# A two-layer attention and retention encoder: the first group's side work in half-round places, the prologue's list in another order, the first rotation read from PSUM

## The chip, the core and the metric

The kernel runs on one core of one Trainium2 chip. Its engines work side by side, each through its own instructions in order: TensorE (PE) multiplies matrices into PSUM, ScalarE (ACT) applies functions, VectorE (DVE) and GpSimd (POOL) do elementwise work, and SyncE (SP) issues the transfers. The metric is the device time of one execution in microseconds (us), lower is better. The kernel is built with its order of instructions written out by the program for PE, ACT, DVE and POOL; the order of SP is written out in the prologue and the first group's first part, and planned by the compiler behind it.

## What is computed

```python
def hybrid_layer(x, norm_gain, w_in, w_out, rel_bias, cos, sin):
    hn = rms_norm(x, norm_gain)
    proj = hn @ w_in.astype(hn.dtype)
    aq, ak, av, ag, rq, rk, rv, rg = jnp.split(proj, cuts, axis=-1)
    ya = chunked_rel_attention(aq..., ak..., av..., rel_bias)      # 8 heads of 64, 9 chunks of 64
    yr = chunkwise_retention(rq..., rk..., rv..., cos, sin)        # 4 heads of 128, decaying state
    y = jnp.concatenate([ya * jax.nn.silu(ag), yr * jax.nn.silu(rg)], axis=-1)
    return x + y @ w_out.astype(x.dtype)

def reference(x, positions, norm_gain, w_in, w_out, rel_bias, final_gain):
    cos, sin = rotary_tables(positions, RET_HEAD_DIM)
    for layer in range(DEPTH):                                     # 2 layers
        x = hybrid_layer(x, norm_gain[layer], w_in[layer], w_out[layer], rel_bias[layer], cos, sin)
    return rms_norm(x, final_gain)
```

x has 2048 rows of 1024 floats; `w_in` is 1024 x 4096 in each layer, `w_out` 1024 x 1024. Before retention, q and k are rotated by tables of cosine and sine that depend on the position: `rotated = t * cos + swapped halves of t * sin`.

## The kernel before

Every float operand of a product is split into two 16-bit parts, and three of the four part products are formed, so that a projection of 128 columns is 24 matmuls per 512 tokens. A layer is cut into four head slices s (two attention heads and one retention head each) and, within a slice, into four groups n of 512 tokens. A group (l, s, n) has two stages. `dense_T` makes attention q, attention k, retention q and retention k with the columns on the partitions (j = 0 to 3); `dense_V` makes the values and gates with the tokens on the partitions (blocks a = 0 to 3). Both write a block of 24 matmuls into one of two PSUM buffers (psD); ACT and DVE empty it (`evacuate`, `rests`), and a buffer must be empty before the block after next begins. A stage has twelve rounds: in each, eight matmuls of the stage, and then one of the three pieces of one unit of the attention of the group before. Work that follows a round is put off by `later(k, fn)`, which runs fn at the start of the k-th round behind; `rests`, the two roundings of the state (`upper_of`, `rest_of`) and the steps of the rotations go this way.

Side work runs beside the stages. It is written as generators that are advanced by `pull` (a step at a time), in `run`, at the end of each round, with as many steps in a round as spread the rest evenly over what is left of the stage. In the first slice this is: the normalized and transposed rows of the tokens (`Tok` for the tiles 0 to 7, `norms_from_input` for the tiles 8 to 15), the cosine and sine tables of the later groups (`tables`, 19 steps, with a Sin on ACT in the middle that needs another function table than the attention's exp), and the split weights of the next slice (`prep_T`, `prep_V`). A token tile's steps are: load, squares with their sum (`sq`, ACT), the root (`root`, a small one on DVE and a power on POOL), the product with the gain (`mul`, 128x1024 on POOL), the upper part (`hi`, ACT), the rest (`lo`, DVE) and two transposing transfers (`dma`, SP).

Ahead of the first rounds stands the prologue, a written list of step names (the call of `do` at L1388): x stands for the first tiles (xsq, xrs, xmul, xtr on TensorE, xhi, xlo), W for the weights of dense_T, V for those of dense_V, t for a step of the first table, u for one of the second, d for a step of dense_T of group (0,0,0), Tu and Vu for small scale columns.

The rotation of a retention q or k is at L663 to L704: ACT copies PSUM to SBUF (`raw`), two transfers swap its halves into `swp`, DVE multiplies `raw` by the cosines and `swp` by the sines and adds, and three more steps make the 16-bit parts. In the first group the k swap is put off by eight rounds.

## Time and profile before

| what | value |
|---|---|
| median of 3 runs (lowest, highest) | 2077.76 us (2076.31, 2078.71) |
| the profiled execution | 2076.73 us, its span 2074.9 us |
| TensorE busy | 2001.0 us, 96% |
| VectorE, ScalarE, GpSimd busy | 1347.7, 1143.1, 462.8 us |
| mean granted clock of TensorE | 0.993 |
| waits of TensorE for DVE's `mbg`, `mbh`, `xa`, at the very start | 5.3, 1.8, 3.8 us |

The profile's rows give a start in us from the span's start, a duration, the engine, the line of the program and what is written from what; a bracket holds how long the engine had stood idle and what ended that. In the rows by stretch, each engine's busy time stands with its count of instructions, and PEclk is the mean granted clock. A row of waits gives the total, how often, and the longest. "PE dV" is dense_V, "PE dT" dense_T, "S" the attention's scores, "r" the retention's products, "gt" the gate, the last of a block that DVE takes out of PSUM.

### The profile page before, as it was taken

To read this page: it belongs to the slowest core of one execution; us is meant where nothing else is said; L and a number is where in the kernel's file an instruction comes from. 1 tells how busy PE (TensorE), PEld (TensorE's weight loads), DVE (VectorE), ACT (ScalarE), POOL (GpSimd) and SP (SyncE) were. 2 spreads that over 40 slices of the span, in tenths; PEclk is the share of its full clock that TensorE was granted. 3 is DMA by queue.
4 is the path that set the end of the run, shared out by engine and by line. 5 is a ranking of instruction groups with operands and counts; after the bars stand their busy time and mean duration, and the time that the engine had idled before them with its cause. 6 is when DMAs were issued, how large, how long until landed. Compare 5 with 4: busy or idle time off the path is not lost. (4 is left out here: it accounts for less than half of the span.)

```text
span 2074.9 us, 39558 instructions
## 1 busy us (share of the span) xinstructions
PE 2001.0 (96%) x14014; PEld 1048.7 (51%) x14014; DVE 1347.7 (65%) x4015; ACT 1143.1 (55%) x2526; POOL 462.8 (22%) x521
## 2 busy tenths in 40 slices
PE   6888999999999999999999999999999999999998
PEld 4444454555555555544444555555555555555543
DVE  7777666666657666676654666666666576667643
ACT  7556665556565654555444546554655665456432
POOL 2233221222122222221000222222222222222100
PEclk9999999999999999999999999999999999999999
DMA  8758674557477754699964556655755877567874
GB/s 253 185 116 172 135 166 109 113 113 161 110 167 138 157 145 101 139 227 266 214 182 111 120 102 140 134 121 101 150 123 127 174 151 162 121 126 176 214 202 123
DMA packets 645574, 313.65 MB, mean 151 GB/s; under 512 B 459104, under 2 KB 601952, under 8 KB 645376
## 3 DMA queue, kind: packets, MB, share of 16 engines
q1 hardware_dynamic: 645376, 311.12, 67.1%
q8 instruction: 110, 1.80, 0.4%
q14 instruction: 88, 0.72, 0.1%
HBM read 123.26 MB, written 41.98 MB: 80 GB/s over the span
## 5 line engine op out<-in xcount | busy, mean ns | idle before, releaser
L812 POOL TENSOR_TENSOR pq<-sc,pq 128x640 f16<-128x640 f32 (+4 forms) x256 | 323.6, 1264 | 1154.1 <-issue 621.4
L809 ACT ACTIVATE sc<-sc,mq,cT 128x640 f32<-128x640 f32 (+4 forms) x256 | 218.5, 853 | 544.7 <-DVE mq L808 409.1
L754 PE MATMUL dV<-whV,hTh 128*128 128x512 f16 x1024 | 354.0, 381 | 8.8 <-DVE gt L772 8.8
L733 PE MATMUL dT<-hTh,whT 128*128 128x512 f16 x1008 | 347.8, 380 | 9.1 <-DMA hTh<-hTl 6.4
L754 PE MATMUL dV<-whV,hTl 128*128 128x512 f16 x1024 | 354.1, 381 | 0.0
L754 PE MATMUL dV<-wlV,hTh 128*128 128x512 f16 x1024 | 353.6, 381 | 0.0
L733 PE MATMUL dT<-hTl,whT 128*128 128x512 f16 x1008 | 346.6, 379 | 0.2 <-DMA hTl<-rln 0.2
L733 PE MATMUL dT<-hTh,wlT 128*128 128x512 f16 x1008 | 346.6, 379 | 0.0
L754 PEld LDWEIGHTS <-hTh 128*128 128x128 f16 x2048 | 197.0, 98 | 222.4 <-DVE gt L772 11.5
L733 PEld LDWEIGHTS <-whT 128*128 128x128 f16 x2016 | 192.6, 98 | 215.4 <-issue 17.5
L806 DVE CUSTOM_DVE_ANT_0 sc<-S,bias 128x640 f32<-128x640 f32 (+4 forms) x256 | 188.3, 736 | 68.3 <-PE S L803 59.0
L811 ACT ACTIVATE pq<-sc 128x640 f16<-128x640 f32 (+4 forms) x256 | 171.5, 670 | 9.8 <-DMA pT<-pq 1.8
L1131 PE MATMUL dO<-whO,yly 128*128 128x512 f16 x448 | 169.8, 379 | 2.5 <-DMA yly<-rly 1.6
L1131 PE MATMUL dO<-whO,yhy 128*128 128x512 f16 x448 | 169.8, 379 | 0.1
L1131 PE MATMUL dO<-wlO,yhy 128*128 128x512 f16 x448 | 169.8, 379 | 0.0
L754 PEld LDWEIGHTS <-hTl 128*128 128x128 f16 x1024 | 99.7, 98 | 104.7 <-issue 2.2
L733 PEld LDWEIGHTS <-wlT 128*128 128x128 f16 x1008 | 97.2, 98 | 101.5 <-issue 0.9
L802 PE MATMUL S<-k,q 128*128 128x128 f16 (+3 forms) x592 | 142.6, 267 | 1.0 <-DVE mq L806 0.9
L822 PE MATMUL o<-v,pT 128*128 128x65 f16 x1120 | 130.0, 194 | 10.0 <-DMA pT<-pq 9.9
L1131 PEld LDWEIGHTS <-yhy 128*128 128x128 f16 x896 | 87.2, 98 | 101.2 <-DMA yhy<-hTh 0.8
L823 PE MATMUL o<-v,pT 128*128 128x64 f16 x1120 | 130.1, 195 | 0.0
L822 PEld LDWEIGHTS <-pT 128*128 128x128 f16 x1120 | 105.6, 97 | 48.4 <-DMA pT<-pq 20.2
(361 smaller groups left out, 3464.2 us busy)
## 6 DMA issues: line engine op xcount, KB each, us to landing
q<-qq SPq DMA_DIRECT2D x128, 128.0 KB, 2.7
yyy<-y_d SPq DMA_DIRECT2D x32, 512.0 KB, 4.6
stT<-in_w_in_dram SPq DMA_DIRECT2D x27, 512.0 KB, 4.9
stV<-in_w_in_dram SPq DMA_DIRECT2D x26, 512.0 KB, 4.7
k<-kk SPq DMA_DIRECT2D x128, 64.0 KB, 2.0
swp<-rot SPq DMA_DIRECT2D x64, 128.0 KB, 2.5
tabc<-tab SPq DMA_DIRECT2D x32, 256.0 KB, 2.7
tabs<-tab SPq DMA_DIRECT2D x32, 256.0 KB, 2.9
```

The source lines that it names most:

```text
L733: pe.matmul(ps, w_[:, j, kt, :], h_[:, kt, :], start=(m == 0), stop=(m == 23))
L754: pe.matmul(ps, h_[:, kt, a * P:(a + 1) * P], w_[:, kt, :], start=(m == 0), stop=(m == 23))
L802: pe.matmul(o, st.q[:, hx, 0, cs], k_, start=True, stop=False)
L806: dve.tensor_tensor_reduce(out=v, in0=S[:, 0:w], in1=g.bias[hx][:, 640 - w:640], scale=1.0, scalar=-3.0e38, op0=ALU.add, op1=ALU.max, accu ...
L809: act.activation(v, v, AF.Exp, bias=m[:, 0:1], scale=g.c[:, 0:1])
L811: act.activation(pq[:, 0:w], v, AF.Copy)
L812: pool.tensor_tensor(pq[:, w:2 * w], v, pq[:, 0:w], op=ALU.subtract)
L822: pe.matmul(o[:, 0:65], u.p[:, b, :], v_[:, 0:65], start=(b == 0), stop=False)
L823: pe.matmul(o[:, 0:64], u.p[:, b, :], v_[:, 65:129], start=False, stop=False)
L1131: pe.matmul(ps, h_[:, kt, :], w_[:, kt, :], start=(m == 0), stop=(m == 23))
```

## The change

The first slice's side work no longer runs in pulls. A table PLAN names, for each piece of work, the half-rounds at which its steps run: half-round 2r is the start of round r, behind the put-off work and ahead of the attention's piece, and 2r+1 its end. Rounds are counted from dense_V of (0,0,0): 0 to 11 are that stage, 12 to 23 dense_T of n=1, 24 to 35 its dense_V, and so on to 84 to 95, dense_T of the first group of the next slice. `run` gets None in place of a number of rounds in these stages, and then pulls nothing.

```diff
+PLAN = {
...
+    "X6": [2, 3, 3, 12, 12, 16],
+    "X7": [1, 2, 7, 7, 10, 14],
...
+    "t1": [4, 6, 8, 12, 15, 15, 16, 16, 18, 18, 24, 24, 26, 27, 28, 29, 29],
+    "t2": [39, 43, 46, 48, 50, 50, 52, 54, 56, 58, 60, 62, 69, 69, 70, 71, 74],
+    "t3": [77, 87, 89, 91, 93, 95, 97, 100, 101, 104, 107, 108, 110, 112, 113, 113, 116],
...
+    "tok12": [69, 76, 77, 77, 84, 86, 87],
+    "tok13": [75, 83, 84, 88, 91, 92, 95],
+    "tok14": [80, 87, 88, 89, 92, 92, 101],
+    "tok15": [91, 97, 99, 99, 100, 107, 108],
+    "prep": [115, 117, 119, 121, 123, 123, 125, 127, 130, 132, 132, 134, 136, 136, 141, 141, 142, 144, 146, 148,
...
+FIRST = (
+    "xsq0 xrs0 t t t xmul0 Wsq0 t t t xtr0 xhi0 Wlp0 Wsc0 xsq1 xlo0 xrs1 xmul1 Whi0 Wlo0 xsq2 xsq3 "
+    "xrs3 xtr1 t d Wsq1 Wlp1 xhi1 xrs2 t xmul2 Wsq2 xlo1 xtr2 xhi2 t xlo2 Wsc1 Whi1 Wsq3 t xmul3 d d "
...
     def run(gen, att, thirds):
         left = thirds
         for _ in gen:
             tick()
+            for fn in slots.pop(2 * ring["round"], ()):
+                fn()
             if att[0] is not None and next(att[0], att) is att:
                 att[0] = None
             ring["att_done"] = att[0] is None
+            for fn in slots.pop(2 * ring["round"] + 1, ()):
+                fn()
+            ring["round"] += 1
+            if left is None:
+                continue
...
-    do("xsq0 xrs0 t xmul0 t t t t xtr0 Wsq0 xhi0 Wlp0 Wsc0 xsq1 xlo0 Whi0 xrs1 xsq2 Wlo0 t xsq3 xmul1 d Wsq1 xrs2 xrs3 xtr1 "
-       "t t xhi1 Wlp1 xmul2 Wsc1 Wsq2 t xtr2 xlo1 xhi2 d Whi1 t xlo2 Wsq3 xmul3 d r Vsq0 Wlp2 Wlo1 t Wsc2 xtr3 Vsq1 r d xhi3 "
...
```

The first group's rotation takes both products out of PSUM: DVE multiplies by the cosines from there, and, a half of the partitions at a time, by the sines with the halves swapped as they are written. The copy by ACT and the swapping transfers fall away there, and only there; k's steps follow q's two rounds behind.

```diff
+        def first_rotation(j, ps, rot):
...
+            def cosine():
+                dve.scalar_tensor_tensor(out=own, in0=ps, scalar=2.0 ** -16, in1=st.tabc, op0=ALU.mult, op1=ALU.mult)
+
+            def sine(half):
...
+                i_, o_ = slice((1 - half) * 64, (2 - half) * 64), slice(half * 64, half * 64 + 64)
+                dve.scalar_tensor_tensor(out=st.swp[o_], in0=ps[i_], scalar=-2.0 ** -16, in1=st.tabs[i_], op0=ALU.mult,
+                                         op1=ALU.mult)
...
+            d = 2 * j
+            later(d, cosine)
+            later(d, lambda: sine(0))
+            later(d + 1, lambda: sine(1))
+            later(d + 2, lambda: dve.tensor_tensor(own, own, st.swp, op=ALU.add))
```

Small edits hold in the whole kernel: products of 128x1 columns become multiplications by a column, the sum of two partial sums and its rounding become one instruction, and the state's 16-bit parts are made one round earlier.

```diff
-                dve.tensor_tensor(rl, rl, g.ka, op=ALU.mult)
+                dve.tensor_scalar(rl, rl, g.ka[:, 0:1], None, op0=ALU.mult)
...
-                later(2, lambda sh=sh, ns=ns: upper_of(sh, ns))
-                later(3, lambda sh=sh, ns=ns: rest_of(sh, ns))
+                later(1, lambda sh=sh, ns=ns: upper_of(sh, ns))
+                later(2, lambda sh=sh, ns=ns: rest_of(sh, ns))
```

**DVE in the prologue.** First before, then now, from the first token's sum (ssn) to the first weights' rounded sum (mbW); xa is the first token tile, wk the first table's working tiles.

```order
L209 TENSOR_SCALAR ssn_0_244<-ssn_0_244,gm_231,ge_232 128x1
L99 CAST wk_163<-wk_166 128x256
L100 TENSOR_SCALAR wk_163<-wk_163,invf_sb 128x256
L256 SCALAR_TENSOR_TENSOR xa<-xa,rsn_0_247,gb_160 128x1024
L96 TENSOR_SCALAR wk_164<-wk_163 128x256
L97 TENSOR_SCALAR wk_164<-wk_164 128x256
L93 SCALAR_TENSOR_TENSOR wk_163<-wk_164,wk_163 128x256 x3
L1269 CAST mbW_270<-m1W_239 128x1
```

```order
L244 TENSOR_SCALAR ssn_0_244<-ssn_0_244,gm_231,ge_232 128x1
L135 CAST wk_163<-wk_166 128x256
L136 TENSOR_SCALAR wk_163<-wk_163,invf_sb 128x256
L132 TENSOR_SCALAR wk_164<-wk_163 128x256
L133 TENSOR_SCALAR wk_164<-wk_164 128x256
L129 SCALAR_TENSOR_TENSOR wk_163<-wk_164,wk_163 128x256
L291 SCALAR_TENSOR_TENSOR xa<-xa,rsn_0_247,gb_160 128x1024
L129 SCALAR_TENSOR_TENSOR wk_163<-wk_164,wk_163 128x256 x2
L143 TENSOR_SCALAR wk_166<-wk_164 128x256
L144 TENSOR_TENSOR wk_166<-wk_166,wk_163 128x256
L1335 CAST mbW_272<-m1W_239 128x1
```

Three table instructions moved ahead of the token's scaling, and two more ahead of mbW.

**SP in the first dense_V.** First before, then now: the transposes of tokens 5 to 7 (hTh_1 and hTl_1 are the second group's rows) up to the bias tile of the second head.

```order
L235 DMA_TRANSPOSE hTh_1_148<-hTl_2_151 128x8x128
L236 DMA_TRANSPOSE hTl_1_149<-hTl_2_151 128x8x128
L1197 DMA hTh_3_152<-in_x_dram 128x1024
L668 DMA swp_0_0_3_902<-raw_0_0_779 64x512
L669 DMA swp_0_0_3_902<-raw_0_0_779 64x512
L235 DMA_TRANSPOSE hTh_1_148<-hTl_2_151 128x8x128
L236 DMA_TRANSPOSE hTl_1_149<-hTl_2_151 128x8x128
L579 DMA bias_1_945<-toep_1_523 128x640
```

```order
L270 DMA_TRANSPOSE hTh_1_148<-hTh_2_150 128x8x128
L271 DMA_TRANSPOSE hTl_1_149<-hTh_2_150 128x8x128
L270 DMA_TRANSPOSE hTh_1_148<-hTl_2_151 128x8x128
L271 DMA_TRANSPOSE hTl_1_149<-hTl_2_151 128x8x128
L270 DMA_TRANSPOSE hTh_1_148<-hTl_2_151 128x8x128
L271 DMA_TRANSPOSE hTl_1_149<-hTl_2_151 128x8x128
L616 DMA bias_1_960<-toep_1_536 128x640
```

The swaps of k and a token load between the last two pairs are gone.

**ACT around the Sin of the third table.** First before (in dense_V of n=1, the second block's evacuation), then now (behind that stage's last one); xb holds the table's tiles, dV the block in PSUM, sc and pq belong to an attention unit.

```order
L918 ACTIVATE state_0_0_1125<-state_0_0_1125 128x128
L204 ACTIVATE hTh_2_150,ssn_11_1447<-hTl_3_153 128x8x128
L121 ACT_TABLE_LOAD
L121 ACTIVATE xb<-xb 128x256
L122 ACTIVATE xb<-xb 128x256
L123 ACTIVATE xb<-xb 128x256
L762 ACTIVATE v_0_1_1299<-dV_0_1_1_1388 128x2x64
L763 ACT_TABLE_LOAD
L763 ACTIVATE gt_0_1_1_1461<-dV_0_1_1_1388,ughV_0_732 128x256
```

```order
L838 ACTIVATE v_0_1_1288<-dV_0_1_3_1550 128x2x64
L839 ACTIVATE gt_0_1_3_1619<-dV_0_1_3_1550,ughV_0_732 128x256
L840 ACTIVATE rv_0_1_3_1618<-dV_0_1_3_1550,urvV_0_730 128x128
L841 ACTIVATE rv_0_1_3_1618<-rv_0_1_3_1618 128x128
L157 ACT_TABLE_LOAD
L157 ACTIVATE xb<-xb 128x256
L158 ACTIVATE xb<-xb 128x256
L159 ACTIVATE xb<-xb 128x256
L942 ACTIVATE dT_0_4_1658<-r_0_4_1601 128x128
L942 ACTIVATE sh_0_3_1642<-state_0_0_1119 128x128
L885 ACT_TABLE_LOAD
L885 ACTIVATE sc_0_1_0_0_1680<-sc_0_1_0_0_1680,mq_0_1_0_0_1681,cT_0_680 128x640
```

The pair of table loads moved from the middle of an evacuation to behind one.

More of the change, by code (lines that the diff above doesn't have):

```diff
@@ L133, in tables @@
         yield
-    TAB_STEPS = 19
     class St:
@@ L659, in evacuate @@
                 rot = b2.tile([P, w, 512], F16, tag=f"rot{j}", name=f"rot{nm}_{j}")
+                if first:
+                    first_rotation(j, ps, rot)
+                    return
                 if j == 2:
@@ L695, in swap @@
                     else:
-                        later(d + 5 if first else 11, tokens)
+                        later(5 if first else 11, tokens)
                 if j == 2:
@@ L1176, in grp, with slot @@
         return groups[l, s]
+    slots = {}
+    ring["round"] = 0
+    def slot(r, fn):
+        slots.setdefault(r, []).append(fn)
     def run(gen, att, thirds):
@@ new lines, in track, with token, load, sq @@
+    def track(name, fns):
+        for h, fn in zip(PLAN[name], fns):
+            slot(h, fn)
+    def token(t, rows):
+        u = St()
+        nm = f"n0_{t}"
+        def load():
+            u.x = w4.tile([P, D], F32, tag="w4", name=f"xin{t}")
+            sp.dma_start(u.x, x[t * P:(t + 1) * P, :])
+        def sq():
+            u.h = [h_[:, :, t % 4 * P:(t % 4 + 1) * P] for h_ in hT_of(0, t // 4)]
+            u.ss = squares(u.x.rearrange("p (k c) -> p k c", c=P), nm, u.h[0])
+        def root():
+            u.rs = rms_of(u.ss, gains[0].m, gains[0].e, nm)
+        def mul():
+            pool.tensor_tensor(u.x, u.x, gains[0].b, op=ALU.mult)
+        track(f"tok{t}", [load, sq, mul, root, lambda: rows_hi(rows, u.x, u.rs), lambda: rows_lo(rows, u.x, u.rs),
+                          lambda: transpose_rows(rows, *u.h)])
@@ L1386, in rounds @@
             yield
-    do("xsq0 xrs0 t xmul0 t t t t xtr0 Wsq0 xhi0 Wlp0 Wsc0 xsq1 xlo0 Whi0 xrs1 xsq2 Wlo0 t xsq3 xmul1 d Wsq1 xrs2 xrs3 xtr1 "
[3 rows of a table removed]
+    do(FIRST)
     g00.vdone = 4
-    push(rounds(["xhi4 xrs5", "xlo4 xrs6 xmul7", "xdma4 xhi5 xrs7 bt", "xlo5 xhi6 u", "xdma5 xlo6", "xdma6 xhi7",
-                 "xlo7", "xdma7 u", "u u bt", "u u bt", "u u", "u u bt"]), 12)
+    for nm, names in TOKEN_STEPS.items():
+        track(nm, [steps[k] for k in names.split()])
+    track("bt", [steps["bt"]] * 4)
+    wk = [[xs0[i][:, k * 256:(k + 1) * 256] for k in range(4)] for i in (2, 3)]
+    t2, t3 = tables(2, wk[0]), tables(3, wk[1])
+    for nm, gen in (("t1", t1), ("t2", t2), ("t3", t3)):
+        track(nm, [lambda gen=gen: next(gen, None)] * 17)
+    for t in range(8, 16):
+        rows = late[t - 8] if t < 12 else xs0[t % 2]
+        v = rows.bitcast(F16)
+        token(t, (v[:, 0:D], v[:, D:2 * D]))
+    prep = PLAN["prep"]
+    slot(prep[0], lambda: push(prep_T(0, 1, grp(0, 1)), 25))
+    track("prep", [lambda: pull(1)] * 48)
     att = [None]
@@ L1444, in hybrid_trunk @@
                     later(11, lambda n=n, g=g, st=st: decayed(l, s, n, g, st, 0))
[L1445 removed]
+                run(dense_V(l, s, n, g, st), att, None if (l, s) == (0, 0) and n else 24 if n == NS - 1 and s < NSW - 1 else 12)
                 if first:
```

124 lines of the change are left out of this document (55 added, 69 removed), and 12 rows, old and new, of tables (FIRST, PLAN, steps).

## The prediction

> **What bounds the kernel now.** I read the page first (TensorE is busy for 2001.0 of 2074.9 us), then the busy time by stretch, then TensorE's waits in the first 300 us, then the timeline around each long wait.
>
> ```profile
> core 0: us, PE busy (x) PEld busy (x) DVE busy (x) ACT busy (x) POOL busy (x), PEclk, DMA share, GB/s
> 20.00:40.00 20.00, 17.97 (x225) 14.71 (x224) 18.98 (x45) 18.38 (x34) 0.84 (x2) 1.00 0.88 277
> 60.00:80.00 20.00, 13.59 (x59) 5.77 (x58) 14.05 (x36) 6.75 (x15) 0.64 (x5) 0.83 0.93 233
> 120.00:140.00 20.00, 16.24 (x92) 7.63 (x91) 11.91 (x35) 13.77 (x32) 6.19 (x5) 0.83 0.70 145
> 180.00:200.00 20.00, 15.73 (x99) 7.88 (x97) 15.85 (x38) 13.69 (x28) 6.22 (x5) 0.83 0.80 178
> 450.00:500.00 50.00, 50.00 (x398) 27.48 (x397) 34.42 (x113) 32.78 (x74) 12.37 (x14) 1.00 0.74 159
> ```
>
> From 400 us on TensorE is all but full; what can be won lies in the first group, where it has gaps and the granted clock falls to 0.83. These are its waits up to 300 us (total, times, longest):
>
> ```profile
> PE dV L754 <- DVE gt L772: 7.8, 4, 3.8
> PE dT L733 <- DMA hTh<-hTl: 6.4, 1, 6.4
> PE r L862 <- DVE sh L870: 3.7, 2, 1.9
> PE msT L325 <- DVE mbT L318: 3.3, 3, 1.9
> PE msV L325 <- DVE ya L834: 2.8, 2, 1.6
> PE dT L733 <- DMA hTh<-rhn: 2.7, 1, 2.7
> ```
>
> These six make 26.7 us, all behind the prologue. In order of time, with the idle time in brackets:
>
> ```profile
> 47.65 1.89 PE L754 MATMUL dV<-whV,hTh 128*128 128x512 f16 x8
> 74.94 3.17 PE L733 MATMUL dT<-hTh,whT 128*128 128x512 f16 x8 [6.41 <-DMA hTh<-hTl]
> 108.19 0.32 PE L802 MATMUL S<-k,q 128*128 128x384 f16 x1 [0.86 <-DVE mq L806]
> 114.35 0.22 PE L862 MATMUL r<-sh,rot 128*128 128x128 f16 x1 [1.83 <-DVE sh L870]
> 115.33 0.61 PE L754 MATMUL dV<-whV,hTh 128*128 128x512 f16 x1 [0.54 <-DVE gt L772]
> 126.71 0.61 PE L754 MATMUL dV<-whV,hTh 128*128 128x512 f16 x1 [3.76 <-DVE gt L772]
> 178.06 0.22 PE L862 MATMUL r<-sh,rot 128*128 128x128 f16 x1 [1.91 <-DVE sh L870]
> 189.97 0.40 PE L754 MATMUL dV<-whV,hTh 128*128 128x512 f16 x1 [2.93 <-DVE gt L772]
> 351.51 0.29 PE L862 MATMUL r<-rv,dT 128*128 128x128 f16 x2 [2.16 <-DVE m2T L327]
> ```
>
> Behind the long gaps the same matmul is slower: eight take 3.17 us at 74.94 and 1.89 at 47.65, one takes 0.61 at 126.71. A mean clock of 0.83 over 20 us is 6.8 us at half speed, so the three stretches hold some 20 us of it (and 100 to 120 us, at 0.91, 3.6). Where the array worked in them, half was lost: about 1.3 us in the first, 1.6 in the one at 115, 2.7 in the one at 125 (5.5 of its 6.8 us were work), 3.4 in the two of the last. With the gaps 9.0 us are at stake for the clock.
>
> Two causes stand behind the gaps at 108 to 190. One is the GpSimd multiplication of a token tile, which holds up DVE:
>
> ```profile
> 110.86 2.35 POOL L1208 TENSOR_TENSOR hTl<-hTl,gb 128x1024 f32<-128x1024 f32 x1
> 110.99 2.51 DVE L93 SCALAR_TENSOR_TENSOR xb<-xb 128x256 f32<-128x256 f32 x1
> 109.50 0.42 DVE L93 SCALAR_TENSOR_TENSOR xb<-xb 128x256 f32<-128x256 f32 x1
> 175.58 2.43 DVE L870 SCALAR_TENSOR_TENSOR sh<-sh,state 128x128 f16<-128x128 f16 x1
> 184.95 2.61 DVE L672 TENSOR_TENSOR raw<-raw,swp 128x512 f32<-128x512 f32 x1
> ```
>
> The same table step takes 0.42 us alone and 2.51 beside GpSimd; the state's rest, 2.43, is the very instruction that TensorE awaits at 178. The other is the Sin of the next table, between a block of dense_V and its evacuation:
>
> ```profile
> 121.23 1.28 ACT L121 ACT_TABLE_LOAD   x1
> 122.84 0.40 ACT L122 ACTIVATE xb<-xb 128x256 f32<-128x256 f32 x1
> 123.72 1.28 ACT L763 ACT_TABLE_LOAD   x1
> 126.25 0.41 DVE L772 SCALAR_TENSOR_TENSOR gt<-gt,dV 128x256 f32<-128x256 f32 x1
> ```
>
> Two loads, three copies of the table through ACT, and the PSUM buffer comes free at 126.66, 0.05 us before TensorE goes on.
>
> **Part 1: up to the first dT of n=1 (74.94 now).** TensorE waits for token 7's transpose, queued on SP behind the swaps of the first k rotation:
>
> ```profile
> 68.55 0.50 SPq L668 DMA_DIRECT2D swp<-raw  x1
> 71.40 2.41 SPq L236 DMA_TRANSPOSE hTl<-hTl  x1
> 36.92 0.68 DVE L636 SCALAR_TENSOR_TENSOR qq<-dT,qq 128x512 f16<-128x512 f32 x1
> 59.57 0.68 DVE L672 TENSOR_TENSOR rot<-rot,tabc 128x512 f32<-128x512 f32 x1
> 11.41 0.29 DVE L97 TENSOR_SCALAR wk<-wk 128x256 f32<-128x256 f32 x1
> 9.89 1.28 DVE L256 SCALAR_TENSOR_TENSOR xa<-xa,rsn,gb 128x1024 f32<-128x1024 f32 x1
> 50.84 2.19 DVE L409 TENSOR_TENSOR reV<-reV 128x1 f32<-128x1 f32 x1
> ```
>
> The swaps (four transfers) and two ACT copies go. In their place DVE reads PSUM three times for each of q and k (cosine, two half sines). No row has this form; the nearest, the rest of q read from PSUM, takes 0.68 us, as much as a rotation step from SBUF. Bounds: 0.34 for a half sine if half the partitions took half the time, 0.68 if not; I take 0.68, since the length per partition is 512 in both. That is 2 x 0.68 more DVE time than two multiplications each, and k's whole rotation moves ahead, from dT of n=1 into the first dense_V.
>
> The prologue pays first. In the new order a rounding of two instructions and one table step stand ahead of the first token's scaling (now at 9.89): 0.29+0.29+0.42 = 1.0 us later. Token 1's transposes stand ahead of the first dense matmuls, and W1's scale is sixth instead of third behind them. Lined up by the rows' durations, DVE being 95% busy from 20 to 40 us, dense_V starts about 2 us later than 47.65; the bounds are 0 (the prologue's slack takes it) and 3. Behind it DVE has up to block 3's evacuation, in the new list: four token rests (1.28 as the scaling, same shape), four evacuations (three instructions, 0.41 at most), ten rotation steps (0.68), eleven table steps (0.42 at most) and 1 us of small ones: 5.1+4.9+6.8+4.6+1 = 22 us. From 49.6 with some 3 us of waits for ACT this ends near 74 (now 77.5), and block 2's evacuation, whose buffer dT of n=1 takes, near 71.5. Two reciprocal chains lose the hold by GpSimd (2.19 us for a 128x1 product). Token 6 is now last on SP; its rest ends near 68, and a pair of transposes is there some 3.5 us after its issue (now 71.40 to 74.94). So dT starts near 72: **-2.9 us**, and with half of the 1.3 us for the clock **-3.5** (bounds +5.3, below, and -9: the whole gap, its clock, and a prologue 1 us shorter).
>
> **Part 2: n=1 and n=2.** The work stays the same, eight multiplications of 2.35 us and three pairs of loads of 1.28. What moves is where it falls. The Sin of table t3 goes ahead of block 3's evacuation in dense_V of n=2, that of t2 (at 121 above) behind the last evacuation of n=1, so that the next one is due a whole block (24 matmuls, 8 of them 1.89 us, and the attention's) later; ACT's load, three copies, second load and one unit's exp (0.85, below) take 1.28+1.2+1.28+0.85 = 4.6 us, which fits under 5.2. Three of tokens 12 to 15's four multiplications fall in dT, where DVE frees a buffer with one instruction and not three; two did before. The state's halves are made one round earlier. At stake for n=1: 0.86+1.83+0.54+3.76 and 1.6+2.7 of clock = 11.3; for n=2: 1.91+0.54+2.93 and 3.4 = 8.8. I take three quarters of both, because each place is still in line on a busy DVE: **-8.5 and -6.6**. Bounds: a quarter, and all.
>
> A rule bears on the clock, and it would shrink this part. By the Trainium skill ("TensorE: Matmul & The Clock Gate", HAM clock gate) the clock halves after an idle window of about 3.4 us. Here it halved behind gaps of 1.83+0.54 and 1.91+0.54 us too; the trace decides. By the page alone those two stretches would cost nothing and the part would be some 2.5 us smaller.
>
> **Part 3: the rest.** Token 15's transposes are issued at half-round 108, six rounds ahead of dT of n=3 (120): the wait of 2.7 us for them goes, **-2.7** (0 to -2.7). The next weights' 48 steps come in places of their own from half-round 115 to 189; 3.3+2.8 us of waits for their sums and the 2.16 at 351, from the same steps' backlog, make 8.3; half of it, **-4.1**. The 128x1 products become multiplications by a column (the first row is the exp above, its mean in ns before the second bar; the others give min, median and max):
>
> ```profile
> L809 ACT ACTIVATE sc<-sc,mq,cT 128x640 f32<-128x640 f32 (+4 forms) x256 | 218.5, 853 | 544.7 <-DVE mq L808 409.1
> L829 DVE TENSOR_TENSOR rl<-rl,kaV x256: 159/159/1329, 92.1 to 1952.3; 128x1 f32<-128x1 f32 x128
> L808 DVE TENSOR_SCALAR mq<-mq,ncT x256: 212/214/217, 79.1 to 1941.0; 128x1 f32<-128x1 f32 x128
> ```
>
> The new form is 0.05 us longer but never held (212 to 217 ns), the old one up to 1.33 us. Over 256 units that is 256 x 0.214 = 54.8 us of DVE for 59.0: nothing for the end, since DVE is covered by TensorE from 400 us on; bounds +2 and -2 for the 20 us of gaps that TensorE still has there.
>
> A rule speaks against it. The Trainium skill ("SBUF — State Buffer", the shared port pair) holds a VectorE instruction in a two-port mode as well as one with two SBUF inputs while GpSimd works. A 128x1 multiplication by a column would be held if it ran in that mode; the 256 rows above show none that was. By the rule in that reading part 1 would be 2 us smaller.
>
> **Sum.** -3.5 -8.5 -6.6 -2.7 -4.1 = -25.4; I add 2.4 for new gaps, three like the 0.86 us one: **-23 us**. The profiled execution took 2076.73 us (its span and 1.8 around it), so 2053.7; the median of the runs is 1.0 higher: **2055**.
>
> **Rivals.** *Gaps move rather than close* (0.17): all of the DVE, GpSimd and ACT work remains, and a place a round off stops the same in-order engine. For it: the DVE's lateness, 2.5 us in one instruction, is as long as a round. Against: in the list by time nothing stands between 126.71 and 178.06, and dT of n=2, to which work moves, lies there. A third of -25.4 remains: 2069.
>
> *Nearly everything closes* (0.12): 26.7 us of the six waits, 0.86 and 2.16 and 9.0 of clock are 38.7; less 2 for the prologue: 2041.
>
> *DVE fails in the first dense_V* (0.10): three PSUM reads for two multiplications, k's rotation moved ahead and a prologue 3 us late leave DVE behind for the whole of n=1. It decides if dT of n=1 starts after 76. Price: start at 79 (+4), 1.3 more of clock, none of n=1's gaps closed and each of the four evacuations there 1.5 us late (+6); half of n=2 and part 3 won (-6.7). +4.6: 2082.
>
> *The places don't do what they say* (0.01): the order shows that they do.
>
> **How the numbers follow.** The forecast has 0.60; its own range is 2045 to 2064. With the rivals on both sides the range is 2041 to 2070. A measurement of this kernel can tell 0.2%, 4.2 us. Faster: 0.60+0.12 and 0.14 of the first rival's 0.17 = 0.86; the same: 0.02 of it and the last rival, 0.03; slower: the third and its last 0.01, 0.11.
>
> **What would show it.** Right: dense_V starts at 48 to 50 and the first dT of n=1 at 71 to 73; no wait over 1.5 us for gt between 100 and 200 us; the clock at 1.00 in 120:140 and 180:200; hTh<-rows waits gone at n=3. Wrong: a first dT after 76, new waits for sh or gt behind the same GpSimd multiplications, waits for pT where ACT stands behind a root, or gaps after 400 us that the small edits made.

## The result, and the profile after

| kernel | median, us (lowest to highest, runs) |
|---|---|
| before | 2077.34 (2076.31 to 2078.71, 4) |
| changed | 2055.22 (2054.70 to 2057.44, 4) |

The ratio is 0.9895, with a 95% interval of 0.9878 to 0.9912: 22.1 us, or 1.1%, faster. The profiled execution of the changed kernel took 2055.64 us, its span 2053.9 (2074.9 before).

TensorE's waits of the changed kernel behind the prologue, up to 300 us (engine, what waited, what ended it: total, times, longest; one of 0.6 for `pT`, the transposed probabilities of an attention unit, is left out):

```profile
PE dV L830 <- DVE gt L848: 5.1, 3, 2.5
PE dT L809 <- DVE xb L129: 2.8, 1, 2.8
PE msV L364 <- DVE mbV L354: 2.4, 1, 2.4
PE msT L364 <- DVE mbT L352: 1.8, 1, 1.8
PE S L878 <- DVE mq L882: 1.7, 1, 1.7
PE dT L809 <- DVE xa L143: 1.2, 1, 1.2
PE dV L830 <- ACT whV L371: 1.1, 1, 1.1
```

The waits for the state's `sh` and both for the transposes of tokens 7 and 15 are gone, and the five waits for the weights' sums are two. Six waits of 1.6 us and more are left behind the prologue (the S of 1.67 and the msT of 1.81 among them). The timeline shows where:

```profile
72.64 1.89 PE L809 MATMUL dT<-hTh,whT 128*128 128x512 f16 x8 [1.20 <-DVE xa L143]
116.61 0.39 PE L830 MATMUL dV<-whV,hTh 128*128 128x512 f16 x1 [2.06 <-DVE gt L848]
126.16 1.89 PE L809 MATMUL dT<-hTh,whT 128*128 128x512 f16 x8 [2.83 <-DVE xb L129]
169.69 0.61 PE L830 MATMUL dV<-whV,hTh 128*128 128x512 f16 x1 [2.50 <-DVE gt L848]
261.30 0.16 PE L364 MATMUL msV<-mbV,ones 128*128 128x1 bf16 x1 [2.41 <-DVE mbV L354]
271.08 1.89 PE L830 MATMUL dV<-whV,hTh 128*128 128x512 f16 x8 [1.09 <-ACT whV L371]
```

The first row was 74.94 and 3.17 us long. The busy time by stretch (us, PE busy, PEld, DVE, ACT, POOL, clock, share of the transfers, GB/s):

```profile
20.00:40.00 20.00, 18.42 (x234) 16.62 (x233) 16.97 (x44) 14.56 (x24) 0.93 (x2) 0.91 0.93 278
60.00:80.00 20.00, 18.26 (x90) 8.23 (x89) 18.79 (x45) 10.83 (x22) 1.27 (x4) 1.00 0.70 137
120.00:140.00 20.00, 17.17 (x122) 8.98 (x121) 12.76 (x43) 15.16 (x33) 8.68 (x8) 1.00 0.84 157
160.00:180.00 20.00, 15.68 (x120) 8.11 (x119) 17.96 (x49) 11.61 (x26) 6.75 (x5) 0.91 0.94 200
180.00:200.00 20.00, 18.10 (x138) 9.44 (x135) 13.34 (x50) 14.76 (x31) 5.20 (x5) 1.00 0.75 169
```

The three stretches that stood at 0.83 are at 1.00; 160 to 180, at 1.00 before, is now at 0.91, behind the wait at 169.69. So is 20 to 40, also at 1.00 before: in this execution the clock fell once in the prologue. In all, the starts of the stages move like this (first matmul of each, from the two traces):

| stage | before | changed | difference so far |
|---|---|---|---|
| dense_V of n=0 | 47.65 | 49.84 | +2.2 |
| dense_T of n=1 | 74.94 | 72.64 | -2.3 |
| dense_T of n=2 | 135.94 | 126.16 | -9.8 |
| dense_T of n=3 | 201.38 | 184.65 | -16.7 |
| dense_T, second slice, n=0 | 259.17 | 239.47 | -19.7 |
| dense_V, second slice, n=0 | 286.95 | 271.08 | -15.9 |
| dense_T, third slice, n=0 | 468.71 | 450.44 | -18.3 |
| last matmul | 2067.58 | 2046.55 | -21.0 |

### The profile page after: what moved, and what is told of

It is laid out like the page before. It is cut to its first block, busy times and chain, and to the rows that moved or that the text cites. A ratio compares the mean times of both kernels' runs of the same rounds, so it can differ in the third digit from the quotient of the medians.

```text
span 2053.9 us, 39511 instructions
## 1 busy us (share of the span) xinstructions
PE 1996.9 (97%) x14014; PEld 1048.2 (51%) x14014; DVE 1292.1 (63%) x4004; ACT 1154.0 (56%) x2524; POOL 459.7 (22%) x521
## 4 chain that ended last, share of the span: by engine, by line
PE 46%; DMA 3%; DVE 3%; ACT 3%; issue 1%; SPq 0%; POOLq 0%; ACTq 0%; DVEq 0%
PE dT L809 14%; PE dV L830 13%; PE dO L1207 12%; PE r L938 2%; PE S L879 1%; PE S L878 1%; DMA pT<-pq 1%; PE o L898 1%; PE o L899 1%; PE o L900 1%; DMA swp<-rot 1%; ACT sc L885 1%; DVE sc L882 1%; ACT pq L887 0%; ACT stO1m L346 0%
## 5 line engine op out<-in xcount | busy, mean ns | idle before, releaser
L878 PE MATMUL S<-k,q 128*128 128x128 f16 (+3 forms) x592 | 142.0, 266 | 1.7 <-DVE mq L882 1.7
L879 PE MATMUL S<-k,q 128*128 128x128 f16 (+3 forms) x592 | 129.3, 266 | 0.0
```

The source lines that it names most:

```text
L878: pe.matmul(o, st.q[:, hx, 0, cs], k_, start=True, stop=False)
L879: pe.matmul(o, st.q[:, hx, 1, cs], k_, start=False, stop=True)
```

## The experiments

The kernels ran on several chips, where the kernel before had medians of 2078.2 to 2079.6 us; so each is compared by its ratio to the kernel before on the same chip. As the intervals are some 0.13% to either side (2.7 us), the table has the profile's parts too: the prologue (up to dense_V of n=0), the stretch from there to the third slice (468.71 before, 450.44 changed), and the rest up to the last matmul. Each kernel has one profile. Parts of the stretch repeat well: dense_T of n=1 to dense_T of n=2 takes 53.52 us in the changed kernel and 53.53 and 53.55 in two experiments that leave it alone (weights spread as before; sums earlier), and from there to dense_V of n=3 it is 86.9 us, and 87.5 and 86.8 in two that leave that part alone (old list; sums earlier). So less than 1 us of the stretch tells nothing. The rest repeats worse: from the third slice on, the order is the same in the changed kernel and in three of the others (old list, Sin in the block, both), yet it takes 1596.1, 1599.9, 1594.7 and 1601.1 us. Most of that difference stands in TensorE's waits for `pT` there: 4.4, 7.7, 4.1 and 8.8 us.

| kernel | ratio (95%) | prologue | stretch | rest |
|---|---|---|---|---|
| before | 1 | 47.6 | 421.1 | 1598.9 |
| changed | 0.9895 (0.9878 to 0.9912) | 49.8 | 400.6 | 1596.1 |
| changed, old list | 0.9901 (0.9887 to 0.9914) | 48.4 | 401.3 | 1599.9 |
| changed, old rotation | 0.9911 (0.9898 to 0.9925) | 48.5 | 406.1 | 1598.8 |
| changed, old products | 0.9897 (0.9882 to 0.9912) | 48.2 | 400.8 | 1596.8 |
| changed, state's halves as before | 0.9920 (0.9907 to 0.9932) | 48.2 | 405.0 | 1599.7 |
| changed, weights spread as before | 0.9909 (0.9895 to 0.9922) | 49.9 | 405.7 | 1598.7 |
| changed, Sin in the block | 0.9902 (0.9887 to 0.9917) | 49.8 | 402.5 | 1594.7 |
| before, halves earlier | 0.9977 (0.9968 to 0.9987) | 48.6 | 418.9 | 1596.1 |
| before, no multiplications | 0.9954 (0.9941 to 0.9966) | 47.7 | 411.7 | 1601.0 |
| before, no Sin | 0.9970 (0.9957 to 0.9984) | 47.6 | 417.8 | 1597.6 |
| changed, two tokens earlier | 0.9896 (0.9883 to 0.9910) | 48.2 | 397.6 | 1598.4 |
| changed, sums earlier | 0.9893 (0.9880 to 0.9907) | 48.4 | 399.9 | 1598.0 |
| changed, both | 0.9876 (0.9857 to 0.9895) | 48.5 | 395.3 | 1601.1 |

### The two causes, each taken from the kernel before

```diff
         def mul(k):
-            pool.tensor_tensor(us[k].x, us[k].x, gains[0].b, op=ALU.mult)
+            pass
```

> The kernel before, without GpSimd's eight multiplications of tokens 8 to 15 by the gain (those tokens are normalised without it). The reason in the prediction, that they hold VectorE up in n=1 and n=2: the waits for the state's rest (1.83 and 1.91 us) and for S and gt behind them (0.86, 0.54, 2.93) go, and with the clock behind them the stretch from the first dT of n=1 to that of n=3 (74.94 to 201.38, 126.4 us) becomes 5 to 9 us shorter; the time is 2069 to 2073 us. The rival, that VectorE is late from the order of its own work and the holds are only seen beside it: less than 2 us, 2075.5 or more.

```diff
-        act.activation(r, ang, AF.Sin)
-        act.activation(k2, k, AF.Sin)
+        turn = AF.Copy if n > 1 else AF.Sin
+        act.activation(r, ang, turn)
+        act.activation(k2, k, turn)
```

> The kernel before, with Copy instead of Sin for the tables of n=2 and n=3 (those two tables hold no sine and cosine; no table of functions is loaded for them). The reason in the prediction, that the loads beside the Sin hold up the evacuation of dense_V: the 3.76 us wait at 126.71 falls below 1.3, and with the clock behind it (2.7 us in 120 to 140) n=1 becomes 4 to 6 us shorter; n=2 gains 1 to 3; the time is 2068 to 2072 us. The rival, that VectorE's own lateness holds the buffer: less than 2 us, 2075.5 or more.

Without the multiplications, 74.94 to 201.38 becomes 74.58 to 192.67: 118.1 us for 126.4, and all waits for `sh` and S are gone. (2.0 us of the gain lie at the end, where the wait for token 15's transposes falls from 2.72 to 0.71.) TensorE's timeline keeps two long waits in n=1 and n=2:

```profile
122.30 0.44 PE L754 MATMUL dV<-whV,hTh 128*128 128x512 f16 x1 [4.88 <-DVE gt L772]
182.70 0.61 PE L754 MATMUL dV<-whV,hTh 128*128 128x512 f16 x1 [4.37 <-DVE gt L772]
```

Without the Sin it is the other way round:

```profile
114.57 0.22 PE L863 MATMUL r<-sh,rot 128*128 128x128 f16 x1 [1.82 <-DVE sh L871]
124.08 0.39 PE L755 MATMUL dV<-whV,hTh 128*128 128x512 f16 x1 [0.81 <-DVE gt L773]
134.50 3.57 PE L734 MATMUL dT<-hTh,whT 128*128 128x512 f16 x8 [3.69 <-DVE r L883]
178.46 0.22 PE L863 MATMUL r<-sh,rot 128*128 128x128 f16 x1 [1.91 <-DVE sh L871]
188.99 0.61 PE L755 MATMUL dV<-whV,hTh 128*128 128x512 f16 x1 [3.13 <-DVE gt L773]
```

The wait of 3.76 us is down to 0.81, as expected, but the 4 to 6 us did not come: TensorE reaches n=2's dense_T sooner and stands there for 3.69 us, and its eight matmuls take 3.57 us at the lower clock. n=1 gains 1.3 us, n=2 1.1. The last wait of n=2 is there without the Sin (3.13) and without the multiplications (4.37); a kernel without both was not run, so what makes it stays open. Both causes are shown, of unequal worth: 8.3 us and 2.4 us of this part.

### The Sin's place in the changed kernel

```diff
-    "t2": [39, 43, 46, 48, 50, 50, 52, 54, 56, 58, 60, 62, 69, 69, 70, 71, 74],
+    "t2": [39, 43, 46, 48, 50, 50, 52, 54, 56, 58, 60, 62, 63, 64, 65, 66, 67],
```

> The changed kernel with the last five steps of table t2 moved seven to three rounds ahead (half-rounds 63 to 67 instead of 69 to 74), so that its Sin lies between the third block of dense_V of n=1 and that block's evacuation, as it did before. The reason in the prediction: a wait of 2.5 to 4 us for gt comes back near 116 to 126 us, the clock falls behind it, and n=1 becomes 3 to 6 us longer: 2057.5 to 2061 us. The rival, that VectorE's lateness counts and not the place of the loads: within 1 us of 2055.2.

TensorE's timeline, and then ScalarE's:

```profile
116.53 0.39 PE L830 MATMUL dV<-whV,hTh 128*128 128x512 f16 x1 [2.21 <-DVE gt L848]
125.89 1.89 PE L809 MATMUL dT<-hTh,whT 128*128 128x512 f16 x8 [2.62 <-DVE yr L1003]
135.87 0.20 PE L898 MATMUL o<-v,pT 128*128 128x65 f16 x1 [2.00 <-DMA pT<-pq]
271.11 2.88 PE L830 MATMUL dV<-whV,hTh 128*128 128x512 f16 x8 [2.74 <-ACT whV L371]
```

```profile
121.16 0.46 ACT L839 ACTIVATE gt<-dV,ughV 128x256 f32<-128x256 f32 x1
122.24 1.28 ACT L157 ACT_TABLE_LOAD   x1
125.95 1.28 ACT L885 ACT_TABLE_LOAD   x1
127.25 0.81 ACT L885 ACTIVATE sc<-sc,mq,cT 128x512 f32<-128x512 f32 x1
```

The waits for `gt` are as in the changed kernel (2.06) or gone; the loads came behind the third block's Tanh (121.16) all the same, and made the attention's exp late: the new wait of 2.00 us is for a transposed `pq`. It costs next to nothing in sum: n=1 takes 53.4 us for 53.5, and n=2 58.9 for 58.5. The stretch is 1.9 us longer all the same, but that comes later, in the second slice, where TensorE waits 2.74 us for `whV` (1.09 in the changed kernel) and the eight matmuls behind it take 2.88 us at the lower clock (1.89 there); why `whV` came later stays open. So the expectation failed. The run does not repeat the place that the Sin had in the kernel before; it tells only that the loads five half-rounds sooner cost nothing in n=1 and n=2. (Where the expectation says rounds, half-rounds are meant.)

### Parts of the change undone

The list, in its old order (the steps that it held then leave PLAN):

```diff
-    "xsq0 xrs0 t t t xmul0 Wsq0 t t t xtr0 xhi0 Wlp0 Wsc0 xsq1 xlo0 xrs1 xmul1 Whi0 Wlo0 xsq2 xsq3 "
+    "xsq0 xrs0 t xmul0 t t t t xtr0 Wsq0 xhi0 Wlp0 Wsc0 xsq1 xlo0 Whi0 xrs1 xsq2 Wlo0 t xsq3 xmul1 "
...
-    "X4": "xlo4 xdma4",
+    "X4": "xhi4 xlo4 xdma4",
...
-    "X6": "xsq6 xmul6 xrs6 xhi6 xlo6 xdma6",
-    "X7": "xsq7 xmul7 xrs7 xhi7 xlo7 xdma7",
+    "X6": "xrs6 xhi6 xlo6 xdma6",
+    "X7": "xmul7 xrs7 xhi7 xlo7 xdma7",
```

> The changed kernel with the prologue's old list (and with it token 4's rounding and the squares of tokens 6 and 7 and token 6's product back in the list). The reason in the prediction: the new list costs about 2 us at the start and pays nothing by itself. Then dense_V of n=0 starts near 47.7 us instead of 49.84, the first dT of n=1 near 70.5 instead of 72.64, and the time is 2052 to 2053.5 us. The rival: the new list is what clears VectorE's way in the first dense_V; then dense_V starts near 47.7 too, but the first dT of n=1 not before 72.5, and the time is 2055 or more.

Neither came out. dense_V starts at 48.43, dense_T of n=1 at 71.11, but the new list started dense_V at 48.2 to 48.6 in six of its nine profiles and at 49.8 to 49.9 in three, the changed kernel's among them. Those three are the ones in which the clock fell in the prologue: 0.91 over 20 to 40 us, and 1.00 in the six (the twelve matmuls of `rlr`, at 29.3 us, take 2.53 us in the changed kernel and 1.48 with the sums earlier). The old list, in five, started dense_V at 47.6 to 48.6 (in the run above the clock fell too, 0.91). By the medians (48.46 and 47.70) the new list costs 0.8 us at the start, and the other 1.4 of the changed kernel's 2.2 go with the clock; the stretch is 0.7 us longer without the new list. So the list is worth too little to show, either way.

The rotation:

```diff
-                if first:
-                    first_rotation(j, ps, rot)
-                    return
...
-                        later(5 if first else 11, tokens)
+                        later(d + 5 if first else 11, tokens)
```

> The changed kernel with the old first rotation (two copies by ScalarE, four swap transfers, multiplications from SBUF). The reason in the prediction: the first dT of n=1 waits for token 7's transposes behind the swaps on the queue, and the rotation from PSUM removes that; then that dT starts 2 to 3 us later than 72.64, behind the transposes of a token, and the time is 2057 to 2059 us. The rival: the places of tokens 4 to 7 alone did it, since their last transposes are issued at half-round 16 in any case; then the first dT of n=1 starts within 0.7 us of 72.64 and the time is within 1.5 us of 2055.2.

```profile
73.00 3.57 PE L806 MATMUL dT<-hTh,whT 128*128 128x512 f16 x8 [3.57 <-DMA hTh<-hTl]
```

That dense_T starts 0.4 us later than 72.64, which by itself is inside the rival's 0.7. But the changed kernel's own start carries the lost clock of its prologue. The five other kernels with the new list and the new rotation whose clock stayed at 1.00 there start it at 70.97 to 71.40; against these, this one, at 1.00 too, is 1.6 to 2.0 us late, and it waits for token 7's transposes again. It is also 2.7 us longer (73.00 to 98.72 for 72.64 to 95.63), with its eight matmuls at the lower clock. The stretch is 5.5 us longer, the largest of the parts undone: 1.7 up to that start, 2.7 in that dense_T, 1.0 in n=2 and n=3.

The products (so in all four places that the change touched):

```diff
-                dve.tensor_scalar(rl, rl, g.ka[:, 0:1], None, op0=ALU.mult)
+                dve.tensor_tensor(rl, rl, g.ka, op=ALU.mult)
```

> The changed kernel with the 128x1 products as tensor by tensor again (the exponent of the scales, the reciprocal chain of V, rl in the attention, y's scale). The reason in the prediction: they lie beside TensorE's work, so the time stays within 1 us of 2055.2. The rival: the holds by GpSimd (up to 1.33 us for the product of rl) are what made the later parts of the program 2.8 us longer before; then the time is 2056.5 to 2058.5 us, and the difference grows from dT of the second slice's second group (346.23 us) to the end, with waits for pT and o behind the products.

The holds are back (the product of `rl` takes up to 1.33 us again, 0.22 at most in the changed kernel), yet the stretch takes 0.2 us more, the rest 0.7, less than the rest differs by without an edit, and the ratio is 0.9897: nothing that shows, as the reason had it. The ratio alone, uncertain by 3 us, would not shut out the rival.

The state's halves:

```diff
-                later(1, lambda sh=sh, ns=ns: upper_of(sh, ns))
-                later(2, lambda sh=sh, ns=ns: rest_of(sh, ns))
+                later(2, lambda sh=sh, ns=ns: upper_of(sh, ns))
+                later(3, lambda sh=sh, ns=ns: rest_of(sh, ns))
```

> The changed kernel with the state's two halves one round later, as before. If the earlier halves are what keeps the retention's matmuls from waiting for sh (1.83 and 1.91 us before): one or two waits of 1 to 2 us for sh come back in n=1 or n=2, with the clock 2 to 6 us, and 1 to 3 us more after 350 us; the time is 2058 to 2063. The rival: it was the places of GpSimd's multiplications, the halves lie a round ahead of their use anyway; then the time stays within 1 us of 2055.2.

```profile
168.41 0.22 PE L938 MATMUL r<-sh,rot 128*128 128x128 f16 x1 [2.01 <-DVE sh L946]
174.34 0.20 PE L898 MATMUL o<-v,pT 128*128 128x65 f16 x1 [3.06 <-DMA pT<-pq]
```

The wait for `sh` is back in n=2, with one for `pT` behind it; the stretch is 4.4 us longer (n=2 takes 62.7 us for 58.5). The converse, the kernel before with these two lines alone:

> The kernel before with one part of the change alone: the state's two halves one round earlier. The changed kernel without it was 5 us slower. If that gain stands by itself: the waits for sh of 1.83 and 1.91 us in n=1 and n=2 go with the clock behind them and 4 to 6 us are won (0.9971 to 0.9981 of the kernel before). The rival, that it needs the places (in the kernel before the GpSimd multiplication holds the rest in whichever round it stands): less than 2 us, 0.999 or more, with waits for sh of over 1.5 us still there or moved to gt.

Its time is 0.9977, in the expected range, but not for the reason given. The waits for `sh` are gone, yet TensorE waits 3.66 us for `gt` in n=1 and more than before (2.93) in n=2:

```profile
128.43 0.61 PE L754 MATMUL dV<-whV,hTh 128*128 128x512 f16 x1 [3.66 <-DVE gt L772]
190.40 0.61 PE L754 MATMUL dV<-whV,hTh 128*128 128x512 f16 x1 [4.51 <-DVE gt L772]
```

The stretch gains 2.2 us, half of what undoing the edit costs; the other 2.8 of its profile lie in the rest, where profiles differ by that much anyway. So by these profiles half of the edit's worth needs the places.

The next weights:

```diff
-    slot(prep[0], lambda: push(prep_T(0, 1, grp(0, 1)), 25))
-    track("prep", [lambda: pull(1)] * 48)
...
+                    run(dT, att, 10 if n == 0 else 14 if (l, s, n) == (0, 0, NS - 1) else None if (l, s) == (0, 0) else 24)
```

> The changed kernel with the next slice's weights spread as before (counted steps from dT of n=3 on, no places of their own). The changed kernel takes 26.4 us for dense_V of n=3 and 31.6 for dT of the next slice's first group, the one before 27.9 and 27.8. If the places only moved this work later: dense_V of n=3 takes near 27.9 again, the dT near 28, and the time is 2052 to 2055 us. The reason in the prediction, that the places take the backlog of these steps away: the old spread costs 2 to 4 us, with waits of 1.5 to 2 for msT and msV and one near 2.2 in the second slice's first group; 2057 to 2059.

```profile
195.04 0.16 PE L364 MATMUL msT<-mbT,ones 128*128 128x1 bf16 x1 [3.94 <-DVE mbT L352]
```

The places are worth 5.1 us of the stretch. With the old spread dense_T of n=3 takes 35.3 us for 28.4, with three waits for `msT` of 6.1 us together; dense_V of n=3 and the dense_T behind it take 28.0 and 27.5, so the 31.6 of the changed kernel is a loss of the places, paid out of a larger gain.

### What the changed kernel still loses

Its waits of 2.06 and 2.50 us stand behind GpSimd's multiplications of tokens 11 and 15. VectorE's and GpSimd's timelines of the changed kernel:

```profile
112.92 2.65 DVE L748 TENSOR_TENSOR raw<-raw,swp 128x512 f32<-128x512 f32 x1
116.14 0.40 DVE L848 SCALAR_TENSOR_TENSOR gt<-gt,dV 128x256 f32<-128x256 f32 x1
165.86 2.80 DVE L754 TENSOR_TENSOR rot<-rot 128x512 f16<-128x512 f32 x1 [0.24 <-ACT rot L751]
```

```profile
111.39 1.14 POOL L888 TENSOR_TENSOR pq<-sc,pq 128x384 f16<-128x384 f32 x1 [4.36 <-issue]
112.49 2.53 POOL L1301 TENSOR_TENSOR xin<-xin,gb 128x1024 f32<-128x1024 f32 x1
164.41 1.40 POOL L888 TENSOR_TENSOR pq<-sc,pq 128x640 f16<-128x640 f32 x1 [11.32 <-issue]
165.76 2.35 POOL L1301 TENSOR_TENSOR xin<-xin,gb 128x1024 f32<-128x1024 f32 x1
```

Both multiplications had been queued on GpSimd behind an attention unit's subtraction.

```diff
-    "tok11": [46, 54, 55, 57, 61, 64, 68],
+    "tok11": [46, 53, 54, 55, 58, 60, 62],
...
-    "tok15": [91, 97, 99, 99, 100, 107, 108],
+    "tok15": [91, 95, 96, 97, 100, 107, 108],
```

> The changed kernel with tokens 11 and 15 one to six half-rounds earlier (token 11's square, multiplication, root, halves and transposes at 53, 54, 55, 58, 60, 62 instead of 54, 55, 57, 61, 64, 68; token 15's first three at 95, 96, 97 instead of 97, 99, 99), so that neither GpSimd multiplication stands behind an attention unit's subtraction just ahead of an evacuation. The theory that the holds by these two multiplications (2.65 and 2.80 us for a VectorE instruction of 0.68, at 112.9 and 165.9 us) make the waits for gt of 2.06 and 2.50 us, and token 11's lateness the 2.83 us at 126.16: these three shrink to under 1 us each, with half the clock behind the second 5 to 8 us are won, and the time is 0.9856 to 0.9873 of the kernel before (2047 to 2051). The rival, that VectorE is full there and the hold only moves to another instruction of its row: waits of the same size for sh, S or gt elsewhere in n=1 and n=2, and less than 2 us won, 0.9887 or more.

```profile
115.07 0.39 PE L830 MATMUL dV<-whV,hTh 128*128 128x512 f16 x1 [0.83 <-DVE gt L848]
165.12 0.39 PE L830 MATMUL dV<-whV,hTh 128*128 128x512 f16 x1 [0.91 <-DVE gt L848]
170.06 0.20 PE L898 MATMUL o<-v,pT 128*128 128x65 f16 x1 [3.04 <-DMA pT<-pq]
```

All three waits shrink as expected. The one at 126.16 is gone: most likely it had been for token 11's transposes (the profile, which infers this, put it down to `xb`). But only 3.0 us of the stretch are won, since 3.04 us are now waited for `pT`; and the time does not tell it from the changed kernel. The theory holds for the waits. The rival's small gain came, but not for its reason: `pT` is no work of VectorE. That transpose lands 7.0 us after its issue, right behind two weight loads of 512 KB, where one issued at 121.30 in the changed kernel lands after 3.2; the changed kernel's own, behind the same loads, takes 6.4 and is not waited for, behind the 2.50 for `gt`.

```diff
-            150, 150, 151, 153, 155, 156, 156, 158, 160, 162, 164, 164, 166, 167, 169, 171, 173, 173, 175, 177,
-            179, 181, 181, 181, 185, 187, 189, 189],
+            150, 150, 151, 153, 155, 156, 156, 158, 160, 162, 164, 164, 166, 167, 169, 171, 173, 173, 175, 176,
+            177, 178, 179, 180, 183, 185, 186, 188],
```

> The changed kernel with the last ten steps of the next slice's weights one to four half-rounds earlier (the square of the last section at 178 instead of 181, its sum at 183 instead of 185, the halves at 183 to 188 instead of 185 to 189). The theory that the places put the last square too late and so cost the next slice's first dT 3.8 us: the wait of 2.41 us for msV at 261.30, the half clock behind it and the 1.09 us for whV at 271.08 go, that dT takes 27.5 to 28.5 us instead of 31.6, and 3 to 4 us are won (0.9875 to 0.9881 of the kernel before). The rival, that ScalarE's row there (three exps, two squares, the bias) is what is late: the waits stay above 1.5 us in sum and less than 1.5 us are won.

The wait for `msV` goes, the dense_T takes 29.2 us, and then TensorE waits 2.6 us for `whV` instead of 1.09. ScalarE's timeline has the reason:

```profile
260.57 0.83 ACT L620 ACTIVATE bias<-bias,ciT 128x640 f32<-128x640 f32 x1 [1.97 <-POOL bias L619]
264.37 1.13 ACT L371 ACTIVATE whV<-stV,sV 128x1024 f16<-128x1024 f32 x1
265.89 1.14 ACT L371 ACTIVATE whV<-stV,sV 128x1024 f16<-128x1024 f32 x1
```

The bias's scaling waits for GpSimd, and the last conversions stand behind it. Net 0.7 us, as the rival had it. So the last kernel puts them ahead, and moves the two tokens too:

```diff
-            150, 150, 151, 153, 155, 156, 156, 158, 160, 162, 164, 164, 166, 167, 169, 171, 173, 173, 175, 177,
-            179, 181, 181, 181, 185, 187, 189, 189],
+            150, 150, 151, 153, 155, 156, 156, 158, 160, 162, 164, 164, 166, 167, 169, 171, 172, 173, 174, 175,
+            176, 177, 178, 179, 181, 183, 184, 186],
```

> The changed kernel with tokens 11 and 15 earlier, as in the run that moved them alone, and the last steps of the next slice's weights earlier again (sum, scale and first half at 181, ahead of the bias's scaling at 182, and the rest at 183 to 186), so that ScalarE does not come to the last conversions behind the bias, which waits for GpSimd. If the two gains add: from the first dense_V to the second slice's second group but one (47.65 to 468.71 in the kernel before, 421.1 us; 400.6 in the changed one, 397.6 with the tokens alone, 399.9 with the sums alone) it takes 395 to 397 us, the wait for whV at the first group of the second slice is under 1.5 us, and the time is 0.986 to 0.988 of the kernel before. The rival, that the second stretch gives back what the first wins (the waits for transposes at 170 us stay, ScalarE's row before 271 us has no more room): 397 to 400 us, and a time of 0.9885 or more, not to be told from the changed kernel's.

The stretch (it ends at the start of the third slice) takes 395.3 us, 5.3 less than in the changed kernel and as expected, with no wait for `whV`; the wait for `pT` stays (3.39 at 170.58). The ratio is 0.9876: faster than the kernel before, and the lowest of all, but its interval overlaps the changed kernel's, and its profile's rest is the longest of all (1601.1). That it beats the changed kernel is likely and not shown.

## Why the prediction was right, and where its terms were off

The time was 2055.0 forecast and 2055.2 measured; the likeliest case came, and none of the rivals (of the first a part: the 2.83 us ahead of dense_T of n=2 were not there before). That the two agree to 0.2 us is luck. The terms that were named, 25.4 us less 2.4 for new gaps, came to 18.3 in the profiles; 2.8 more came from behind the second slice, where nothing was forecast. What held is the direction, the places where the time would be won, and about three quarters of its size. Against the profiles' own 21.0 us:

| term | predicted | came |
|---|---|---|
| up to dense_T of n=1, and its clock | -3.5 | -2.3 -1.3 = -3.6 |
| n=1, without that clock | -8.5 | -6.2 |
| n=2, with token 15 | -6.6 -2.7 = -9.3 | -7.0 |
| the next weights (201.38 to 364.50) | -4.1 | -1.5 |
| new gaps, already inside the rows above | +2.4 | |
| behind that, the small edits | 0 | -2.8 |

*The prologue pays about 2 us*: 2.2 in the two profiles, but 0.8 by the medians of all. The other 1.4 go with the clock, which fell there in the changed kernel's execution and which no term had. *The rotation lifts token 7's transposes out from behind the swaps*: shown (3.57 us of wait come back without it), and worth more than was forecast: where the clock held in the prologue, dense_T of n=1 starts at 70.97 to 71.40 and not at 72. So the first row agrees because two errors cancel. (The forecast's sum for VectorE up to block 3's evacuation ends at 75.0, not near 74; that evacuation ended at 75.87.) Half of the clock's 1.3 us was allowed for, and all of it was won.

*n=1 and n=2, three quarters*: of what was at stake (11.3, and 8.8 with token 15's 2.7), 6.2 and 7.0 came, 55% and 60%. Two of the eight multiplications still met VectorE ahead of an evacuation. In n=1 this is shown to be the shortfall: with both moved, n=1 takes 51.3 us for 53.5. In n=2 it is not: there the wait for `pT` took the place of the one for gt, and n=2 takes 59.1 us for 58.5. "No wait over 1.5 us for gt between 100 and 200 us" failed twice (2.06, 2.50); these are new waits for gt behind the same multiplications, which the prediction had named as a sign of being wrong. The clock at 1.00 in 120:140 and 180:200 held. *The Sin as the second cause* held for the wait that it was read from (3.76 to 0.81) and was over-valued: with it gone the next transposes are waited for, and loads five half-rounds sooner cost nothing in n=1 and n=2 of the changed kernel. *The state's halves one round earlier* stood in the prediction as a half-sentence, without a price; undoing them costs 4.4 us of the stretch, a fifth of the change.

*The next weights*: the mis-sized term. The places save 5.1 us against the old spread under the new places; against the kernel before only 1.5 was left, since the last square now came late in the next slice's first dense_T (31.6 us for 27.8: the waits of 2.41 and 1.09 with the lower clock between).

*The products cost nothing* was right (0.2 us). The 2.8 us behind the second slice, which no term foresaw, are not evidence for an edit: kernels with one order there differ by 6.4 us.

Of the 20.5 us of the stretch, undoing one part at a time gives back 5.5 (rotation), 5.1 (weights), 4.4 (halves), 1.9 (Sin, though not in the part that the Sin stands in), 0.7 (list) and 0.2 (products), 17.8 in all. What the token places of n=1 and n=2 do by themselves was not tried, and the parts need not add.

## What to carry to other kernels

A long multiplication on GpSimd is best placed by what VectorE will run while it lasts: the holds of 2.0 and 2.1 us ahead of a PSUM evacuation made 1.2 and 1.6 us of wait there, while the holds of the 128x1 product of `rl`, up to 1.33 us each, cost 0.2 us of the stretch. A wait that is taken away uncovers the next late thing (transposes at 134, `pT` at 170, conversions at 271): of what was at stake, half to six tenths was won here in n=1, in n=2 and with the two tokens (3.0 of 5.7 us), and less with the sums alone (0.7 of 3.5). Until the wait behind it is priced too, a gap is not to be counted in full. Where a program of 2 ms has a part whose time wanders by 6 us, compare the stretch that was changed, from its first to its last stage.

## What the hardware showed beyond that

The length of a gap alone does not decide the clock. In the changed kernel it halved behind 2.50 us at 169.69 (one matmul 0.61) and stayed whole behind 2.83 us at 126.16 (eight in 1.89). Nor does the place: with the sums earlier, the same wait of 2.83 us, ahead of the same matmuls, was followed by the lower clock (eight in 3.44). What differs is how the gap lies in the steps of the clock: up to 2040 us, every stretch at half speed in these traces is 3.41 or 6.83 us long. First the changed kernel, then the sums earlier, each the step with the beginning of that gap and the next one:

```profile
121.74:125.15 3.41, 1.59 (x15) 0.88 (x12) 3.13 (x9) 0.52 (x2) 0.36 (x1) 1.00 0.81 151
125.15:128.57 3.42, 2.41 (x22) 1.37 (x23) 2.59 (x12) 3.29 (x8) 1.16 (x1) 1.00 0.88 189
```

```profile
121.04:124.45 3.41, 0.81 (x11) 0.52 (x9) 3.31 (x11) 0.73 (x1) 0.00 (x0) 1.00 1.01 190
124.45:127.86 3.41, 3.18 (x8) 1.17 (x9) 2.61 (x10) 3.32 (x9) 1.16 (x1) 0.50 0.85 200
```

In the changed kernel the gap is cut in two and TensorE is idle for 1.82 us of the first step; with the sums earlier it is idle for 2.60, and the next step runs at half. Laid out like this from 44 us on, all fourteen profiles agree: at full clock, each of the 46 steps with 2.02 us or more idle was followed by one at half, and no step with 1.96 or less was. (In the prologue the clock fell four times behind 1.4 to 1.9 us.) So the same gap can cost a halved step in one execution and none in the next. A mean of 0.91 over 160 to 180 us is 3.6 us at half speed. The Trainium skill ("TensorE: Matmul & The Clock Gate", HAM clock gate) tells of a free-running window of about 3.4 us, which agrees with the length of that stretch; that a whole window must be idle does not agree with the gap of 2.50.

The hold works both ways and reaches one-input instructions. In the kernel with two tokens earlier, GpSimd's multiplication took 3.24 us for 2.35, and beside it a VectorE instruction with a single SBUF input took 1.26 for 0.28. The Trainium skill ("SBUF — State Buffer", Who interferes with whom) gives the pair of ports that the two share to whichever issues first and blocks the other. The VectorE row at 159.36 agrees. GpSimd's extra 0.89 us does too, if its last 2.35 us, from 158.12 on, are the multiplication: VectorE's step of 157.57, with two SBUF inputs, ran at its usual length until 158.26. But by the rows GpSimd had begun 0.34 us before that step, so which of the two came first can't be read from them. GpSimd's and VectorE's timelines there:

```profile
157.23 3.24 POOL L1301 TENSOR_TENSOR xin<-xin,gb 128x1024 f32<-128x1024 f32 x1 [6.11 <-ACT hTh L239]
```

```profile
157.57 0.69 DVE L748 TENSOR_TENSOR rot<-rot,swp 128x512 f32<-128x512 f32 x1
159.36 1.26 DVE L143 TENSOR_SCALAR xb<-xb 128x256 f32<-128x256 f32 x1
```
